# Keeping six of eight split weight blocks for the last two token tiles of an output product

## The chip, the cores and the metric

The kernel runs on one core of one Trainium2 chip. The metric is the device time of one execution in microseconds, taken as the median of several runs. Five engines work side by side: PE multiplies matrices, ACT and DVE work elementwise, POOL does small leftovers, and SP issues the transfers between HBM and the on-chip memory (SBUF). Each takes its instructions in the order that the built program fixed for it, and waits for the others by semaphores. Products accumulate in PSUM.

## The reference

The reference is a two-layer encoder on 1024 tokens of width 1024 in float32. Layer 0 mixes tokens by two kinds of attention, layer 1 by a gated linear recurrence; both end in a dense gated feed-forward part. The change touches only the last step of each mixer and the norm behind it:

```python
m = concat(out_a, out_b) @ w_out          # layer 0: attn_w_out, 1024 x 1024
m = (hs * gate) @ w_out                   # layer 1: rg_w_out,   1024 x 1024
x = x + rmsnorm(m, norm_mix_post[layer])
h = rmsnorm(x, norm_ffn_pre[layer])
f = (silu(h @ w_gate) * (h @ w_up)) @ w_down
```

Results have to agree with float32 products, so no operand may simply be rounded.

## The kernel before

There are eight token tiles of 128 tokens (0 to 7), and eight weight blocks of 128 x 1024 per `w_out` (one for each 128 rows of the sum).

**Two ways to multiply.** A product of two float32 operands is made in one of two ways. In the first, each operand is cut into a high part (a cast to the `F32R` type, on ACT) and a low part (operand minus high part, on DVE), and PE makes three passes: high x high, high x low, low x high. In the second, PE multiplies the plain float32 rows; the trace then shows two records for each such product of 128 x 512. `split` (L140) cuts a weight block: the cast is L155 (tile `whi`), the subtraction L156 (`wlo`). `split_act` (L581) cuts the activations: L582 (`ah`), L583 (`al`). All products of the stage are recorded on L572.

**The output product, `out_product` (L555).** A first pass makes tiles 0, 1, 2, a second makes tiles 3, 4, 5; each loads and splits all eight weight blocks anew, and keeps three PSUM tiles open at once (`pst`, three buffers, so the second pass can begin only when the tile-0 result has been read out of its buffer). The list `kept` remembers the split parts of the last four blocks of the second pass. Tiles 6 and 7 come last: the four kept blocks in three passes, and then, for tile 6 and after it for tile 7, the other four blocks as plain rows, loaded once more (L634).

**Rings.** Loaded weight blocks go through a ring of three buffers, `raw` (L136): a load waits until the subtraction of the block three before it is done. Split parts go through a ring of eight, `w`, which so holds four blocks. Activations (`act`, `ah`, `al`) have rings of three. The plain rows of the tail and then the first seven weight operands of the feed-forward part (`q`, made by `gate_load`: casts L691, subtractions L692) take the same ring `w` in turn.

**The norm.** When a tile's product is complete, `post_norm_of` squares it (ACT L178, tile `junk`), multiplies by the gain (DVE L250, `mg<-ps`; with that, PSUM is free), takes the root on POOL (`rs`, L182 and L183), adds the residual (DVE L256, `x`), and writes `x` out. `pre_norm` squares that again (ACT L178, `mg<-x`), takes the root on POOL, and scales (ACT L212, `mg<-x,rs`). PE then turns the tile in eight 128 x 128 transposes (L222), and ACT and DVE spread the turned tile into the operands `hS` of the feed-forward part (L85, L89, L96).

**Order.** The engines' order is made when the program is built, by a simulation of the timeline that places each instruction when it would be ready; `behind` adds that an instruction may not be placed ahead of another. So an edit can change the order on all engines. In the tail, the transposes of tiles 3, 4, 5 are placed ahead of the first three plain blocks of tile 6, and the first products of the feed-forward part (`first`, then `strassen`, L721 to L723) fill the time in which tiles 6 and 7 are normed.

## Time and profile before

| | us |
|---|---|
| runs, median of 3 | 2201.48 |
| lowest, highest | 2198.03, 2202.87 |
| the profiled execution | 2197.6 |
| its span, first to last instruction | 2195.8 |
| PE busy | 2161.5 |
| DVE busy | 1540.4 |
| ACT busy | 1170.8 |

The stage of the output product lies at 486 to 600 us for layer 0 and at 1455 to 1569 us for layer 1. A row of the timeline gives start, duration, engine, line, operation, the tiles (out<-in, without their numbers), shapes and a count; what stands in brackets is how long the engine was idle before, and what it waited for. A PE row's duration contains the time in which the next instruction already runs; the pitch of PE is the distance of starts.

### The profile page before, as it was taken

To read this page: it belongs to the slowest core of one execution; us is meant where nothing else is said; L and a number is where in the kernel's file an instruction comes from. 1 tells how busy PE (TensorE), PEld (TensorE's weight loads), DVE (VectorE), ACT (ScalarE), POOL (GpSimd) and SP (SyncE) were. 2 spreads that over 40 slices of the span, in tenths; PEclk is the share of its full clock that TensorE was granted. 3 is DMA by queue.
4 is the path that set the end of the run, shared out by engine and by line. 5 is a ranking of instruction groups with operands and counts; after the bars stand their busy time and mean duration, and the time that the engine had idled before them with its cause. 6 is when DMAs were issued, how large, how long until landed. Compare 5 with 4: busy or idle time off the path is not lost. (4 is left out here: it accounts for less than half of the span.)

```text
span 2195.8 us, 30592 instructions
## 1 busy us (share of the span) xinstructions
PE 2161.5 (98%) x11140; PEld 1802.7 (82%) x11140; DVE 1540.4 (70%) x2526; ACT 1170.8 (53%) x2174; POOL 219.3 (10%) x450
## 2 busy tenths in 40 slices
PE   9999999999999999999999999999999999999998
PEld 8888889878788888888887777888788888888886
DVE  5877865556878777776777677437787777758675
ACT  6655555556765544443446676528754444424443
POOL 2111113121100000000002333102000000000011
PEclk9999999999999999999999999999999999999999
DMA  7101011126323333236458411356233333328565
GB/s 273 34 30 49 24 40 49 54 95 210 137 91 112 123 97 112 89 126 229 145 179 256 131 59 39 95 197 219 90 118 105 100 116 91 117 96 289 171 182 154
DMA packets 168279, 270.21 MB, mean 123 GB/s; under 512 B 13889, under 2 KB 94785, under 8 KB 168129
## 3 DMA queue, kind: packets, MB, share of 16 engines
q1 hardware_dynamic: 167488, 266.18, 37.7%
q10 hardware_dynamic: 640, 2.10, 0.3%
q8 instruction: 87, 1.43, 0.3%
q14 instruction: 64, 0.52, 0.1%
HBM read 202.69 MB, written 65.54 MB: 122 GB/s over the span
## 5 line engine op out<-in xcount | busy, mean ns | idle before, releaser
L722 PE MATMUL ps<-hS,q 128*128 128x512 f32 (+1 forms) x1288 | 490.0, 381 | 0.9 <-DVE hS L89 0.9
L721 PE MATMUL ps<-hS,q 128*128 128x512 f32 (+1 forms) x1288 | 490.3, 381 | 0.4 <-ACT hS L96 0.4
L723 PE MATMUL ps<-hS,q 128*128 128x512 f32 (+1 forms) x1288 | 489.2, 380 | 0.0
L692 DVE TENSOR_TENSOR q<-raw,q 128x512 fp32r<-128x512 f32 x308 | 204.7, 686 | 183.8 <-ACT q L691 183.3
L722 PEld LDWEIGHTS ps<-hS,q 128*128 128x128 f32 x1288 | 242.9, 189 | 47.5 <-DVE hS L89 1.3
L721 PEld LDWEIGHTS ps<-hS,q 128*128 128x128 f32 x1288 | 242.4, 189 | 47.0 <-ACT hS L96 0.8
L723 PEld LDWEIGHTS ps<-hS,q 128*128 128x128 f32 x1288 | 242.9, 189 | 46.1
L691 ACT CAST q<-raw 128x512 fp32r<-128x512 f32 x308 | 177.7, 616 | 160.9 <-DVE raw L700 123.2
L807 PE MATMUL ps<-o,o 128*128 128x512 f32 x616 | 240.0, 390 | 0.2
L808 PE MATMUL ps<-o,o 128*128 128x512 f32 x616 | 238.0, 390 | 0.5 <-DVE o L936 0.5
L679 ACT ACTIVATE raw<-raw,gcol 128x256 f32<-128x256 f32 x352 | 150.3, 498 | 145.1 <-DMA raw<-in_ffn_w_up_dram 77.6
L806 PE MATMUL ps<-o,o 128*128 128x512 f32 x616 | 221.3, 391 | 3.6 <-ACT o L935 2.7
L801 ACT CAST o<-raw 128x512 fp32r<-128x512 f32 x184 | 110.6, 620 | 159.3 <-PE ps L808 56.7
L182 POOL TENSOR_SCALAR rs<-ss 128x1 f32<-128x1 f32 x52 | 25.0, 481 | 1429.1 <-ACT junk L178 1363.7
L802 DVE TENSOR_TENSOR o<-raw,o 128x512 fp32r<-128x512 f32 x184 | 123.3, 687 | 54.8 <-ACT o L801 54.2
L806 PEld LDWEIGHTS ps<-o,o 128*128 128x128 f32 x616 | 115.5, 188 | 30.0 <-ACT o L935 4.5
L808 PEld LDWEIGHTS ps<-o,o 128*128 128x128 f32 x616 | 115.6, 188 | 25.1 <-DVE o L936 1.3
L807 PEld LDWEIGHTS ps<-o,o 128*128 128x128 f32 x616 | 115.7, 188 | 24.9 <-DVE o L802 1.0
L156 DVE TENSOR_TENSOR wlo<-raw,whi 128x1024 fp32r<-128x1024 f32 x76 | 93.3, 1228 | 57.7 <-ACT whi L155 57.0
L409 DVE TENSOR_TENSOR_SCAN pr<-pr,zero 128x128 f32<-128x128 f32 (+7 forms) x64 | 86.9, 1361 | 30.7 <-POOL pr L406 25.7
L155 ACT CAST whi<-raw 128x1024 fp32r<-128x1024 f32 x76 | 79.7, 1050 | 49.2 <-PE ps L167 20.1
L166 PE MATMUL psq<-hT,whi 128*128 128x512 f32 x256 | 101.8, 398 | 0.1
(206 smaller groups left out, 4315.8 us busy)
## 6 DMA issues: line engine op xcount, KB each, us to landing
raw<-in_ffn_w_gate_dram SPq DMA_DIRECT2D x44, 512.0 KB, 4.2
raw<-in_ffn_w_up_dram SPq DMA_DIRECT2D x44, 512.0 KB, 4.2
gS<-c SPq DMA_DIRECT2D x88, 256.0 KB, 3.9
raw<-gS SPq DMA_DIRECT2D x88, 256.0 KB, 2.7
gA<-c SPq DMA_DIRECT2D x66, 256.0 KB, 3.3
raw<-in_ffn_w_down_dram SPq DMA_DIRECT2D x63, 256.0 KB, 4.4
raw<-gA SPq DMA_DIRECT2D x44, 256.0 KB, 2.8
t<-in_ffn_w_down_dram SPq DMA_DIRECT2D x22, 512.0 KB, 6.5
```

Source lines behind the costliest of these rows:

```text
L166: nc.tensor.matmul(ps, wh[:, kt, cols], hh[:, kt, :], start=kt == 0, stop=False)
L679: nc.scalar.activation(raw[:, i], raw[:, i], AF.Copy, scale=gain[:, 4 * k + i:4 * k + i + 1])
L691: self.last = nc.scalar.copy(t[:, 0], src).ins
L692: self.last_lo = nc.vector.tensor_tensor(t[:, 1], src, t[:, 0].bitcast(F32), op=ALU.subtract).ins
L721: nc.tensor.matmul(ps, a[:, 0, kt, :], bh, start=kt == 0, stop=False)
L722: nc.tensor.matmul(ps, a[:, 0, kt, :], bl, start=False, stop=False)
L723: self.matmul = nc.tensor.matmul(ps, a[:, 1, kt, :], bh, start=False, stop=kt == 3).ins
L801: nc.scalar.copy(t[:, 0], src)
L802: tt(t[:, 1], src, t[:, 0].bitcast(F32), op=ALU.subtract)
L806: nc.tensor.matmul(ps, a[0], b[:, 0], start=first, stop=False)
L807: nc.tensor.matmul(ps, a[0], b[:, 1], start=False, stop=False)
L808: nc.tensor.matmul(ps, a[1], b[:, 0], start=False, stop=last)
```

## The change

The second pass puts the split parts of blocks 3 and 4 of its order (`kts[2:4]`) into a new ring of four, `more`, in a pool of its own, and `kept` now remembers every block. Tiles 6 and 7 take the four last blocks as before, then the two blocks of `more` in three passes, with two more activations split for it, and only the first two blocks as plain rows. Two loads of 512 KB per layer fall away. Lines move by one behind L139 and by five or six behind the tail: L155 is L156 in the changed kernel, L178 is L179, L250 is L251, L691 is L696.

```diff
--- before.py
+++ after.py
@@ -137,9 +137,10 @@
         self.last_load = self.nc.sync.dma_start(raw.rearrange("p (a b) -> p a b", a=a), src).ins
         return raw
 
-    def split(self, src, a, b, gain=None, raw=None, pool=False):
-
-        nc, m = self.nc, self.main
+    def split(self, src, a, b, gain=None, raw=None, pool=False, home=None):
+
+        nc = self.nc
+        m, tag, bufs = home or (self.main, "w", 8)
         if raw is None:
             raw = self.raw(src, a)
         if gain is not None and pool:
@@ -150,8 +151,8 @@
             v = raw.rearrange("p (a b) -> p a b", a=a)
             nc.vector.tensor_tensor(v, v, gain.rearrange("p (a o) -> p a o", o=1).to_broadcast([P, a, b]),
                                     op=ALU.mult)
-        hi = m.tile([P, 1024], F32R, tag="w", bufs=8, name=self.uid("whi"))
-        lo = m.tile([P, 1024], F32R, tag="w", bufs=8, name=self.uid("wlo"))
+        hi = m.tile([P, 1024], F32R, tag=tag, bufs=bufs, name=self.uid("whi"))
+        lo = m.tile([P, 1024], F32R, tag=tag, bufs=bufs, name=self.uid("wlo"))
         nc.scalar.copy(hi, raw)
         nc.vector.tensor_tensor(lo, raw, hi.bitcast(F32), op=ALU.subtract)
         return (hi.rearrange("p (a b) -> p a b", a=a),
@@ -552,7 +553,7 @@
     def psum_t(self):
         return self.pt.tile([P, 512], F32, tag="tr", bufs=2, name=self.uid("pst"))
 
-    def out_product(self, ap, pp, first, aT, w, x_src, x_dst, gpost_v, sink, kts):
+    def out_product(self, ap, more, pp, first, aT, w, x_src, x_dst, gpost_v, sink, kts):
 
         nc = self.nc
         wv = [w[kt * P:(kt + 1) * P, :].rearrange("p (a b) -> p a b", a=2) for kt in range(KT)]
@@ -582,7 +583,7 @@
             nc.scalar.copy(ah, a)
             nc.vector.tensor_tensor(al, a, ah.bitcast(F32), op=ALU.subtract)
 
-        gpost, kept = None, []
+        gpost, kept = None, {}
         for t0 in (0, 3):
             pst = [psum() for _ in range(3)]
             for kt in kts:
@@ -595,8 +596,8 @@
                 else:
                     a = act(kt, t0, 3, ap, 3)
                     ah, al = (ap.tile([P, 384], F32R, tag=n, bufs=3, name=self.uid(n)) for n in ("ah", "al"))
-                wh, wl = self.split(wv[kt], 2, 512)
-                kept = kept[-3:] + [(wh, wl)]
+                wh, wl = self.split(wv[kt], 2, 512, home=(more, "more", 4) if t0 and kt in kts[2:4] else None)
+                kept[kt] = wh, wl
                 split_act(a, ah, al)
                 for t in range(3):
                     tok = slice(t * P, (t + 1) * P)
@@ -620,25 +621,29 @@
 
 
         pst = [psum() for _ in range(2)]
-        for i, (kt, (wh, wl)) in enumerate(zip(kts[4:], kept)):
+        def passes(kt):
             a = act(kt, 6, 2, ap, 3)
             ah, al = (ap.tile([P, 384], F32R, tag=n, bufs=3, name=self.uid(n))[:, :2 * P] for n in ("ah", "al"))
             split_act(a, ah, al)
+            wh, wl = kept[kt]
+            return [(ah, wh), (ah, wl), (al, wh)]
+
+        for i, kt in enumerate(kts[4:]):
+            ps_of = passes(kt)
             for t in range(2):
                 tok = slice(t * P, (t + 1) * P)
                 with self.behind([self.matmul] if t else ()):
-                    matmuls(pst[t], [(ah[:, tok], wh), (ah[:, tok], wl), (al[:, tok], wh)], i == 0, False)
-        rows, acts = [], []
-        for i, kt in enumerate(kts[:4]):
+                    matmuls(pst[t], [(x[:, tok], y) for x, y in ps_of], i == 0, False)
+        tail = [passes(kt) for kt in kts[2:4]]
+        for kt in kts[:2]:
             raw = self.main.tile([P, 2, 512], F32, tag="w", bufs=8, name=self.uid("raw"))
             nc.sync.dma_start(raw, wv[kt])
-            rows.append(raw)
-            acts.append(act(kt, 6, 2, ap, 3, ("act", "act", "act", "ah")[i]))
+            tail.append([(act(kt, 6, 2, ap, 3), raw)])
         for t in range(2):
             for i in range(4):
 
                 with self.behind([self.matmul] + ([self.turned[3 + i]] if t == 0 and i < 3 else [])):
-                    matmuls(pst[t], [(acts[i][:, t * P:(t + 1) * P], rows[i])], False, i == 3)
+                    matmuls(pst[t], [(x[:, t * P:(t + 1) * P], y) for x, y in tail[i]], False, i == 3)
             if t == 0:
                 rest = norm(6, pst[0])
                 last_m = self.last_m
@@ -1143,8 +1148,8 @@
         nc.sync.dma_start(self.gcol, io["gcol"])
         with pool("s0") as sp:
             hS = HiddenS(self, sp)
-            with pool("o0", "right") as ap, psum("po0") as pp:
-                self.out_product(ap, pp, lambda *a: first(0, *a), oT,
+            with pool("o0", "right") as ap, pool("more0") as more, psum("po0") as pp:
+                self.out_product(ap, more, pp, lambda *a: first(0, *a), oT,
                                  io["attn_w_out"], x, xs[0], io["norm_mix_post"][0],
                                  hS, [4, 5, 6, 7, 0, 1, 2, 3])
             if stop == 0:
@@ -1168,8 +1173,8 @@
             banks.close()
         with pool("s1") as sp:
             hS = HiddenS(self, sp)
-            with pool("o2", "right") as ap, psum("po2") as pp:
-                self.out_product(ap, pp, lambda *a: first(1, *a), yT,
+            with pool("o2", "right") as ap, pool("more2") as more, psum("po2") as pp:
+                self.out_product(ap, more, pp, lambda *a: first(1, *a), yT,
                                  io["rg_w_out"], xs[1], xs[2], io["norm_mix_post"][1],
                                  hS, list(range(KT)))
             if stop == 2:
```

The edit moves instructions in both layers in the same way. Three places in layer 0 follow; the numbers at the names tell the tiles apart.

On ACT, where the first pass ends. `whi` is a weight block's cast, `ah` an activation's, and `junk<-ps` the squaring of tile 0, with which the reading of the first PSUM tile begins. Before:

```order
L155 CAST whi_5986<-raw_5984 128x1024
L582 CAST ah_5982<-act_5980 128x384
L155 CAST whi_6016<-raw_6014 128x1024
L582 CAST ah_6012<-act_6010 128x384
L155 CAST whi_6046<-raw_6044 128x1024
L178 ACTIVATE junk_5870,ss_5872<-ps_5624 128x1024
```

Now:

```order
L156 CAST whi_5989<-raw_5987 128x1024
L156 CAST whi_6049<-raw_6047 128x1024
L583 CAST ah_5985<-act_5983 128x384
L156 CAST whi_6019<-raw_6017 128x1024
L156 CAST whi_6079<-raw_6077 128x1024
L583 CAST ah_6015<-act_6013 128x384
L156 CAST whi_6109<-raw_6107 128x1024
L179 ACTIVATE junk_5873,ss_5875<-ps_5627 128x1024
```

Ahead of the squaring of tile 0 stood the cast of the second pass's third block; there stands now the cast of its fifth (`raw_6107`), and the third and fourth are cast earlier.

On SP, the loads for these casts. Before:

```order
L137 DMA raw_6044<-in_attn_w_out_dram 128x1024
L562 DMA act_6040<-oT_79 128x384
L137 DMA raw_6074<-in_attn_w_out_dram 128x1024
L562 DMA act_6070<-oT_80 128x384
L137 DMA raw_6104<-in_attn_w_out_dram 128x1024
L562 DMA act_6100<-oT_73 128x384
```

Now:

```order
L137 DMA raw_6047<-in_attn_w_out_dram 128x1024
L563 DMA act_6043<-oT_79 128x384
L137 DMA raw_6077<-in_attn_w_out_dram 128x1024
L137 DMA raw_6107<-in_attn_w_out_dram 128x1024
L563 DMA act_6073<-oT_80 128x384
L137 DMA raw_6137<-in_attn_w_out_dram 128x1024
```

The fifth block's load (`raw_6104`, now `raw_6107`) stands in the same place among the weight loads; only an activation load has gone behind it.

On DVE, between the gain of tile 6 (`mg<-ps`) and its residual (`x<-mg,rs,x`). Before:

```order
L250 TENSOR_TENSOR mg_6454<-ps_6356,g_5865 128x1024
L705 TENSOR_TENSOR raw_6486<-raw_6486,raw_6480 128x4x128
L89 TENSOR_TENSOR hS_5617<-tf_6314,hS_5616 128x16x64
L256 SCALAR_TENSOR_TENSOR x_6455<-mg_6454,rs_6458,x_6455 128x1024
```

Now:

```order
L251 TENSOR_TENSOR mg_6469<-ps_6359,g_5868 128x1024
L710 TENSOR_TENSOR raw_6509<-raw_6509,raw_6503 128x4x128
L697 TENSOR_TENSOR q_6519<-raw_6503,q_6519 128x512
L89 TENSOR_TENSOR tf_6317<-tf_6317,mg_6233 128x256
L697 TENSOR_TENSOR q_6520<-raw_6509,q_6520 128x512
L257 SCALAR_TENSOR_TENSOR x_6470<-mg_6469,rs_6473,x_6470 128x1024
```

Two subtractions of the feed-forward weights and a small step of the turning have come in between, and one larger step (`hS<-tf`) has gone out.

## The prediction

> **What bounds the kernel now.** I read the page's span and busy times first, then the waits of PE.

> ```profile
> span 2195.8 us, 30592 instructions
> PE 2161.5 (98%) x11140; PEld 1802.7 (82%) x11140; DVE 1540.4 (70%) x2526; ACT 1170.8 (53%) x2174; POOL 219.3 (10%) x450
> PE pst L222 <- ACT mg L212: 4.8, 3, 2.0
> PE ps L806 <- ACT o L935: 2.7, 4, 1.2
> ```

> PE is busy all the time, and its longest waits are three for a scaled tile ahead of its transposes, 4.8 us together. So every microsecond taken from PE counts, unless it comes back as a wait, and every new wait of PE counts in full. The timeline of PE at the end of layer 0's stage gives prices:

> ```profile
> 565.15 1.04 PE L222 MATMUL pst<-ident,mg 128*128 128x128 f32 x8
> 566.03 1.88 PE L572 MATMUL ps<-raw,act 128*128 128x512 f32 x4
> 567.75 1.04 PE L222 MATMUL pst<-ident,mg 128*128 128x128 f32 x8
> 568.62 1.88 PE L572 MATMUL ps<-raw,act 128*128 128x512 f32 x4
> 571.21 10.47 PE L572 MATMUL ps<-raw,act 128*128 128x512 f32 x24
> 582.83 0.28 PE L723 MATMUL ps<-hS,q 128*128 128x256 f32 x1
> 585.08 1.09 PE L222 MATMUL pst<-ident,mg 128*128 128x128 f32 x8 [1.98 <-ACT mg L212]
> ```

> Tile 3's transposes start at 565.15; the plain blocks of tiles 6 and 7 follow, then products of the feed-forward part, then 1.98 us of nothing until tile 6 is normed. One plain block of one tile is four records, 567.75 - 566.03 = 1.72 us.

> The other place that matters is the end of the first pass: ACT, DVE, SP and PE, and the landing of a load in the window 512 to 516 and in 520 to 526.

> ```profile
> 510.99 1.05 ACT L155 CAST whi<-raw 128x1024 fp32r<-128x1024 f32 x1
> 514.65 0.52 ACT L582 CAST ah<-act 128x384 fp32r<-128x384 f32 x1 [2.61 <-PE ps L572]
> 515.07 1.05 ACT L155 CAST whi<-raw 128x1024 fp32r<-128x1024 f32 x1
> 516.24 1.02 ACT L178 ACTIVATE junk<-ps 128x1024 bf16<-128x1024 f32 x1
> ...
> 512.07 1.23 DVE L156 TENSOR_TENSOR wlo<-raw,whi 128x1024 fp32r<-128x1024 f32 x1 [0.39 <-ACT whi L155]
> 516.15 1.23 DVE L156 TENSOR_TENSOR wlo<-raw,whi 128x1024 fp32r<-128x1024 f32 x1 [0.40 <-ACT whi L155]
> 517.38 1.23 DVE L250 TENSOR_TENSOR mg<-ps,g 128x1024 f32<-128x1024 f32 x1
> ...
> 513.32 0.33 SPq L137 DMA_DIRECT2D raw<-in_attn_w_out_dram  x1
> ...
> 518.53 0.39 PE L572 MATMUL ps<-whi,al 128*128 128x512 f32 x1
> 518.75 0.41 PE L572 MATMUL ps<-whi,ah 128*128 128x512 f32 x1
> ...
> raw<-in_attn_w_out_dram SPq DMA_DIRECT2D x1, 512.0 KB, 3.7
> raw<-in_attn_w_out_dram SPq DMA_DIRECT2D x1, 512.0 KB, 5.1
> ```

> The second pass's first product (518.75) needs tile 0's PSUM, which DVE frees at 517.38 + 1.23 = 518.61. PE does not wait, but with 0.14 us to spare. The casts repeat every 515.07 - 510.99 = 4.08 us, a block of 18 passes (three tiles, two halves, three), so a pass costs 0.227 us.

> **The change part by part.**

> *PE.* A block of one tile in three passes is six passes, 1.36 us, against 1.72 as plain rows: 0.36 less. Two blocks and two tiles make 1.44 us per layer, 2.9 us in both. That is all the direct gain there is.

> *The loads taken away.* Two of 512 KB per layer; no PE row above waits for them, so they cost nothing now. I price them at 0; the low end would be a wait that the list of PE's waits does not have.

> *The end of the first pass.* ACT takes its queue in order: at 514.65 it had stood 2.61 us for an activation buffer with ready work behind. The third block's cast (515.07) stood ahead of tile 0's squaring (516.24) and waited for nothing. Now the fifth block's cast stands there. Its load, the one issued at 513.32, cannot go sooner: it waits for its buffer, which the subtraction 512.07 to 513.30 frees, and that one follows the cast of 510.99, which still stands behind the activation cast of that block. Landing takes 3.7 us here, so the cast begins at 517.0 instead of 515.07, and the squaring, the new block's subtraction, the gain and the freed PSUM follow 1.9 us later, at about 520.5. PE, which had 0.14 us to spare, stands still for about 1.9 us. Before, the first pass's squarings, gains and residuals lay between this load and its cast and hid it; with that cover gone it is on the path. Bounds: 0 if the load landed by 515, 3.3 with the landing of 5.1 us (513.32 + 5.1 - 515.07). I take 1.9, since 3.7 is this very load's landing, and the other loads now issued close by come behind it. Queued behind the waiting cast are the squarings of tiles 0 and 1; DVE's gain and POOL's root wait for these. What follows on ACT, DVE and POOL moves with PE, by the same amount. One more wait could come of it: the first feed-forward weight's scaling now stands on ACT ahead of the fourth block's activation cast. I take 0 and allow 0.7 at the high end, the difference of the two landings halved.

> *The tail.* Two blocks of tile 6 shrink, so its product ends 0.72 us sooner, and PE has 0.72 us less of tile 7 to cover its norm. When the norm ends decides, since the transposes wait for it already. These rows follow it: ACT, then DVE, then the whole stretch.

> ```profile
> 558.75 0.39 ACT L582 CAST ah<-act 128x256 fp32r<-128x256 f32 x1
> 563.13 1.12 ACT L691 CAST q<-raw 128x512 fp32r<-128x512 f32 x2
> 564.16 1.06 ACT L178 ACTIVATE mg<-x 128x1024 f32<-128x1024 f32 x1
> 567.00 1.15 ACT L212 ACTIVATE mg<-x,rs 128x1024 f32<-128x1024 f32 x1
> 574.85 1.02 ACT L178 ACTIVATE junk<-ps 128x1024 bf16<-128x1024 f32 x1 [0.70 <-PE ps L572]
> 580.52 1.05 ACT L178 ACTIVATE mg<-x 128x1024 f32<-128x1024 f32 x1
> 583.88 1.15 ACT L212 ACTIVATE mg<-x,rs 128x1024 f32<-128x1024 f32 x1 [2.21 <-POOL rs L183]
> ...
> 576.00 1.22 DVE L250 TENSOR_TENSOR mg<-ps,g 128x1024 f32<-128x1024 f32 x1
> 577.14 0.68 DVE L705 TENSOR_TENSOR raw<-raw,raw 128x512 f32<-128x512 f32 x1
> 577.74 1.22 DVE L89 TENSOR_TENSOR hS<-tf,hS 128x1024 fp32r<-128x1024 f32 x1
> 578.87 1.28 DVE L256 SCALAR_TENSOR_TENSOR x<-mg,rs,x 128x1024 f32<-128x1024 f32 x1
> ...
> 566.00:582.00 16.00, 16.00 (x55) 8.25 (x54) 15.69 (x29) 13.01 (x23) 2.00 (x4) 1.00 0.46 179
> ```

> In the last row DVE is busy 15.69 of 16 us and ACT had only 0.70 us of idle before it squared tile 6. The change adds two activation casts to ACT (0.39 each) and two subtractions to DVE. Thus 0.78 of new work eats the 0.70, and a product that ends 0.72 sooner finds ACT still busy. Tile 5's squaring (564.16) also goes behind both casts of the new activations and its scaling (567.00) comes about a microsecond later, with part of ACT's queue behind it. So tile 6's squaring starts 0.1 (0.78 - 0.70) to 0.9 us later than at 574.85; I take 0.5. Then DVE: between gain and residual lay 577.14 to 578.87, 1.73 us; now two weight subtractions of the size of the one at 577.14 (0.60 each, to 577.74) and a step of half that size (0.3, an estimate) replace the 1.13 of the large one (577.74 to 578.87), so +0.4. Scaling and transposes: +0.9 against tile 3's transposes, instead of -0.72. Tile 7's residual now stands behind the large step (1.13), partly covered: +0.3. The tail thus comes out 1.2 us longer per layer, its 1.44 us of PE work turned into idle time before tile 6's transposes (1.98 becomes about 4). Bounds: -1.44 if the norm keeps up with everything, +1.9 with 0.9, 0.4 and 0.6.

> *Sum.* 1.9 + 1.2 = 3.1 us per layer. Layer 1 has the same order and nearly the same rows, so 6.2 in all: 2197.6, the profiled execution, becomes 2203.8. That execution ran 3.9 us under the median of the runs, 2201.48, so I add the 6.2 to the median: 2207.7.

> **The clock.** Behind the 1.98 us gap of layer 0 the granted clock fell; behind the same gap in layer 1 it did not:

> ```profile
> 586.00:590.00 4.00, 4.00 (x23) 4.00 (x22) 3.85 (x4) 3.97 (x8) 0.79 (x2) 0.57 0.19 76
> 1554.00:1558.00 4.00, 4.00 (x36) 4.00 (x35) 3.15 (x3) 3.97 (x9) 0.79 (x2) 1.00 0.20 69
> ```

> With the clock at 0.57, 23 products instead of 36 were begun in 4 us: 13 x 0.11 = 1.4 us lost. A new gap of 1.9 us inside dense work could cost this in each layer, 2.8 in all, by chance of its position; I leave it out of the sum and keep it for the range.

> [...]

> **The rivals.**

> *No stall at the end of the first pass* (0.20). The load lands by 515. For it: landings of about 3.7 leave only 1.9 us to find. Against it: its buffer is freed at 513.30. Then only the tail counts: 2 x 1.2 = 2.4, 2203.9.

> *The tail follows the product* (0.12). The norm keeps its length and starts 0.72 sooner. For it: ACT has waits in the tail that earlier free operand buffers take away. Against it: DVE at 15.69 of 16. With the stall: 2 x (1.9 - 0.72) = 2.4, again 2203.8.

> *Faster* (0.06). One mechanism: operand buffers of the feed-forward part come free before the tail rather than after plain blocks, so the norm gets so short that PE's gap closes. It decides from the point where the norm shortens by more than the 0.72 us of cover that is lost. Then PE's 1.44 and most of the 1.98 us go per layer, without a stall: 2 x -3.4 = -6.8, 2194.7. PE's 2.9 alone would give 2198.6, which is within the bound below.

> *The clock falls too* (0.20, a part of slower). Both stalls fall badly: 6.2 + 2.8 = 9.0, 2210.5.

> **How the numbers follow.** 0.2% of 2201.48 is 4.4 us, about what a measurement of this kernel can tell from no change. The forecast (2207.7, 6.2 slower) has 0.42 and the clock's case 0.20: slower 0.62. The two rivals at +2.4 have 0.32: same. Faster 0.06. The likeliest case's own range is 2204 to 2211. The range for 8 in 10 reaches down over the rivals at +2.4, with the runs' own spread of 2 to 3 us, to 2200.5, and up to the long landing (2 x 3.3 + 2.4 = 9.0) with one fallen clock (1.4) and some spread, 2213.

> **What would show it.** Right: a PE wait for DVE's `mg` of about 1.9 us at the first product of the second pass in both layers; ahead of it on ACT a `whi` cast that waits for the load of a weight block; plain rows x32 instead of x64; tile 6's transposes waiting some 4 us. Wrong: no wait of PE at that product, or a gap before the transposes of 2.7 us or less, which would mean that the norm followed its product.

## The result, and the profile after

The change makes the kernel slower, by little: 2204.74 us (median of 20 runs) against 2198.82 us for the kernel before on the same chip, a ratio of 1.0031 with a 95% interval of 1.0025 to 1.0036. By the medians that is 5.9 us, by the ratio 6.8 (5.5 to 7.9). Forecast was a difference of 6.2, on a median of 2201.48 for the kernel before, so 2207.7. That is 3.0 us too much, of which 2.7 come from the starting point: the median of the first three runs lay that much above the one of 20. The profiled execution took 2202.89 us. Its page begins:

```profile
span 2201.1 us, 30616 instructions
PE 2162.0 (98%) x11156; PEld 1808.3 (82%) x11156; DVE 1541.6 (70%) x2530; ACT 1172.8 (53%) x2178; POOL 219.4 (10%) x450
```

PE idles 2201.1 - 2162.0 = 39.1 us, before 2195.8 - 2161.5 = 34.3: 4.8 more. PE is busy 0.5 us longer, although it has less to do. Where the idle time went, the list of PE's waits says (waited for: us in all, times, longest):

```profile
PE pst L223 <- ACT mg L213: 4.5, 2, 2.5
PE pst L223 <- ACT mg L85: 4.2, 3, 3.1
```

The first row is the old wait, the scaled tile ahead of its transposes. The second is new: transposes that wait for a free PSUM buffer, which a copy on ACT (L85) empties. The rows of PE for the transposes of tiles 3 to 7 show where, layer 0 first, then layer 1; the last number is the idle time ahead. After:

```profile
565.50 1.03 PE L223 MATMUL pst<-ident,mg 128*128 128x128 f32 x8
568.53 1.15 PE L223 MATMUL pst<-ident,mg 128*128 128x128 f32 x8 [0.63 <-ACT mg L85]
571.50 1.14 PE L223 MATMUL pst<-ident,mg 128*128 128x128 f32 x8 [0.43 <-ACT mg L85]
586.23 1.64 PE L223 MATMUL pst<-ident,mg 128*128 128x128 f32 x8 [2.55 <-ACT mg L213]
594.68 1.10 PE L223 MATMUL pst<-ident,mg 128*128 128x128 f32 x8
...
1534.69 1.03 PE L223 MATMUL pst<-ident,mg 128*128 128x128 f32 x8
1536.94 1.03 PE L223 MATMUL pst<-ident,mg 128*128 128x128 f32 x8
1542.47 1.97 PE L223 MATMUL pst<-ident,mg 128*128 128x128 f32 x8 [3.12 <-ACT mg L85]
1558.20 1.10 PE L223 MATMUL pst<-ident,mg 128*128 128x128 f32 x8 [1.97 <-ACT mg L213]
1566.64 1.09 PE L223 MATMUL pst<-ident,mg 128*128 128x128 f32 x8
```

And before, the last of these in layer 0, then the first and the last in layer 1:

```profile
593.25 1.03 PE L222 MATMUL pst<-ident,mg 128*128 128x128 f32 x8
...
1533.85 1.04 PE L222 MATMUL pst<-ident,mg 128*128 128x128 f32 x8
...
1561.43 1.09 PE L222 MATMUL pst<-ident,mg 128*128 128x128 f32 x8 [0.80 <-ACT mg L212]
```

From tile 3's transposes to tile 7's, "the tail" below, layer 0 took 593.25 - 565.15 = 28.10 us and takes 29.18; layer 1 took 27.58 and takes 31.95. Layer 1 carries most of it (4.37 of 5.45 us), by a wait of 3.12 us ahead of tile 5's transposes that layer 0 does not have. The rows of DVE, POOL and ACT there, and the same place in layer 0 (last two rows):

```profile
1536.06 3.23 POOL L183 TENSOR_SCALAR rs<-ss 128x1 f32<-128x1 f32 x1 [4.99 <-ACT mg L179]
...
1538.53 0.68 DVE L705 TENSOR_TENSOR raw<-raw,raw 128x512 f32<-128x512 f32 x1
1541.67 0.69 DVE L89 TENSOR_TENSOR hS<-mg,hS 128x512 fp32r<-128x512 f32 x1 [2.46 <-ACT hS L96]
...
1539.98 1.15 ACT L213 ACTIVATE mg<-x,rs 128x1024 f32<-128x1024 f32 x1 [3.05 <-POOL rs L184]
...
568.09 0.22 POOL L183 TENSOR_SCALAR rs<-ss 128x1 f32<-128x1 f32 x1 [6.17 <-ACT mg L179]
...
568.51 0.92 DVE L89 TENSOR_TENSOR tf<-mg 128x256 f32<-128x256 f32 x2 [0.50 <-ACT mg L85]
```

POOL's operation on 128 x 1 numbers, the first half of the root for tile 5's second norm, takes 0.22 us in layer 0 and 3.23 in layer 1. In layer 1 it ends at 1539.29, right after DVE has run dry (1538.53 + 0.68 = 1539.21); in layer 0 DVE had a pause of 0.50 us just then. ACT's scaling stands for that root, ACT's copies stand behind the scaling, and PE's transposes wait for the copies. A run of DVE without a pause does not always do this, though. In the kernel before, the same operation for tile 5 lay in such a run too and took 0.47 us:

```profile
565.39 0.47 POOL L182 TENSOR_SCALAR rs<-ss 128x1 f32<-128x1 f32 x1 [3.85 <-ACT mg L178]
```

The clock is the second part. In the rows for stretches of the change (length and PE's busy time, products begun, granted clock) the clock is 0.50 in layer 1 too, where before it stayed at 1.00 (in the trace's clock records from 589.8 to 2190.7 us):

```profile
1542.40:1545.80 3.40, 3.33 (x10) 0.50 0.00 0
1545.80:1549.20 3.40, 3.40 (x11) 1.00 0.00 0
1559.40:1562.80 3.40, 3.40 (x19) 0.50 0.00 0
```

With layer 0's fall, which the kernel before has as well (0.50 from 586.4 to 589.8), that is two falls more. At a clock of 0.50, 3.4 us cost 1.7 us, an estimate from these two numbers, so 3.4 in all. The account closes: 4.8 of idle time, 3.4 of clock, and 2.9 less work on PE give +5.3 us, which is the difference of the spans. The runs bear the clock's part out: the mean granted clock of the change's 20 runs is 0.9954, and that of the kernel before is 0.9969 to 0.9971 in the four series of runs beside the experiments. The difference of some 0.0016 is 3.5 us of 2200.

### The profile page after: what moved, and what is told of

Read it like the earlier page. It is cut to its first block, busy times and chain, and to the rows that moved or that the text cites. A ratio compares the mean times of both kernels' runs of the same rounds, so it can differ in the third digit from the quotient of the medians.

```text
span 2201.1 us, 30616 instructions
## 1 busy us (share of the span) xinstructions
PE 2162.0 (98%) x11156; PEld 1808.3 (82%) x11156; DVE 1541.6 (70%) x2530; ACT 1172.8 (53%) x2178; POOL 219.4 (10%) x450
## 5 line engine op out<-in xcount | busy, mean ns | idle before, releaser
L696 ACT CAST q<-raw 128x512 fp32r<-128x512 f32 x308 | 178.3, 616 | 178.4 <-DVE raw L705 131.6
L806 ACT CAST o<-raw 128x512 fp32r<-128x512 f32 x184 | 110.6, 620 | 158.0 <-PE ps L813 47.5
L183 POOL TENSOR_SCALAR rs<-ss 128x1 f32<-128x1 f32 x52 | 26.5, 509 | 1435.1 <-ACT junk L179 1362.9
L156 ACT CAST whi<-raw 128x1024 fp32r<-128x1024 f32 x76 | 79.7, 1050 | 50.1 <-PE ps L168 20.4
## 6 DMA issues: line engine op xcount, KB each, us to landing
raw<-in_ffn_w_gate_dram SPq DMA_DIRECT2D x44, 512.0 KB, 4.1
raw<-in_ffn_w_up_dram SPq DMA_DIRECT2D x44, 512.0 KB, 4.2
t<-in_ffn_w_down_dram SPq DMA_DIRECT2D x22, 512.0 KB, 6.5
```

The lines of the kernel that those rows point to most:

```text
L696: self.last = nc.scalar.copy(t[:, 0], src).ins
L806: nc.scalar.copy(t[:, 0], src)
```

## The experiments

The differences in us below are (ratio - 1) x 2198, with the 95% interval in brackets.

**One layer at a time.** `out_product` exists twice, as before and as changed:

```
 layer 0:  self.out_product(ap, more, pp, ...)      # e1: changed;  e2: as before
 layer 1:  self.out_product_b(ap, pp, ...)          # e1: as before; e2: changed
```

> The change in layer 0 alone; layer 1's output product is as before. Theory S (the root of tile 5 on POOL, held up behind DVE in layer 1, and what follows from it carries the loss): in the profile of the change layer 1 starts only 0.3 us late, so +0 to +1 us against the kernel before, no difference that can be measured. Rival R (the prediction's: each layer loses the same at the end of the first pass and in the tail): half of the change's loss, +3 us.

> The change in layer 1 alone; layer 0's output product is as before. Theory S: the whole loss, +4 to +6 us, with a wait of PE of about 3 us for a copy on ACT (L85) ahead of tile 5's transposes in layer 1, and one POOL operation of some 3 us there. Rival R: +3 us, like layer 0 alone.

Layer 0 alone: +1.3 us [-0.7, 3.3]. Layer 1 alone: +4.4 [2.6, 6.4], with 3.17 us of waiting ahead of tile 5's transposes and 3.24 us for POOL's operation. The intervals do not quite exclude halves; the profiles, with the wait in layer 1 only, speak for theory S.

**Without tile 5's root.** In `pre_norm`, `rstd` returns the plain mean square for tile 5:

```
+        if not root:
+            return ss[-1]
```

> The change in both layers, with the two POOL operations left out that take the root for tile 5's second norm: tile 5 is scaled with its plain mean square, so its numbers are wrong from there, while every other instruction and its order on PE, DVE, ACT and SP is that of the change. Theory S: ACT no longer waits 3.05 us for POOL ahead of tile 5's scaling in layer 1, PE's wait of 3.12 us goes and with it the fallen clock right behind it (about 1.4 us): +0.5 to +2 us against before. Rival R: the root of tile 5 is beside the path, so the loss stays, +5 to +6 us.

```profile
1537.58 1.03 PE L225 MATMUL pst<-ident,mg 128*128 128x128 f32 x8
1539.84 1.03 PE L225 MATMUL pst<-ident,mg 128*128 128x128 f32 x8
1542.26 1.14 PE L225 MATMUL pst<-ident,mg 128*128 128x128 f32 x8
1556.99 1.09 PE L225 MATMUL pst<-ident,mg 128*128 128x128 f32 x8 [2.55 <-ACT mg L215]
1565.43 1.09 PE L225 MATMUL pst<-ident,mg 128*128 128x128 f32 x8
```

These are tiles 3 to 7 in layer 1. The wait is gone, and the tail takes 1565.43 - 1537.58 = 27.85 us, within 0.3 of the kernel before. But the time was +5.5 us [3.1, 7.9], where 0.5 to 2 had been expected. So the root accounts for the tail of layer 1 and not for the whole loss. The mean granted clock of these runs is 0.9954, as low as the change's, and 0.9970 for the kernel before beside them, so about 3.5 of the 5.5 us lie in the clock, and leaving out the root did not bring them back. What else stands in this profile is a wait of 1.3 us for the gain at the end of layer 1's first pass: the prediction's third step, which the one profile of the change had shown with 0.28 us only. It was in every profile that has the change's loads in layer 1. In the run with a product put ahead (e6, below) it looked like this, by rows of ACT, of PE, and of a stretch of time:

```profile
1485.30 1.05 ACT L156 CAST whi<-raw 128x1024 fp32r<-128x1024 f32 x1 [2.36 <-DMA raw<-in_rg_w_out_dram]
...
1488.79 0.80 PE L573 MATMUL ps<-whi,ah 128*128 128x512 f32 x1 [2.61 <-DVE mg L251]
...
1488.20:1495.00 6.80, 6.21 (x15) 0.50 0.71 259
```

There ACT stood 2.36 us for the fifth block's load ahead of tile 0's squaring, PE 2.61 us, and then the clock was at 0.50 for 6.8 us, which costs another 3.1 by estimate (half of the 6.21 us of work in them).

**The sums of the weights later, and the first half alone.** The first puts three sums on DVE behind tile 4's differences, so that DVE pauses. The second (e5) keeps the blocks in their own buffers, with the tail of the kernel before.

```
 e4: +        with self.behind([self.gap] if behind else ()):
                  tt(a22, a21, a22, op=ALU.add)      # and the two behind it
 e5: -        tail = [passes(kt) for kt in kts[2:4]]
     +        rows, acts = [], []                    # four blocks as plain rows
```

> The change, with the three sums of the first feed-forward weights (L703 to L705 of the change) put on DVE behind tile 4's differences, and what depends on them behind tile 6's norm: DVE then runs dry for a moment after tile 3's transposes, as in layer 0 of the change. Theory S: POOL's root gets through there, the wait ahead of tile 5's transposes goes in layer 1, and tile 6's norm finds ACT and DVE freer: 3 to 6 us less than the change, -1 to +2 us against before. Rival R: sums that come later delay the weights' parts, so nothing is won, +5 us or more.

> The first half of the change alone: the second pass keeps the parts of its third and fourth block in buffers of their own, so the ring's buffers come free earlier, and the tail is that of the kernel before, with four blocks as plain rows. Theory S (the end of the first pass costs little; the tail's new casts and subtractions on ACT and DVE carry the loss): a wait of PE for the gain of 0.3 to 1.4 us at the end of layer 1's first pass, as in the four profiles with the change there, none in layer 0, no wait of 3 us ahead of tile 5's transposes; 0 to +2 us against before. Rival E (earlier weights alone crowd DVE: the feed-forward weights' parts come earlier and hold up tile 5's root): +3 to +5 us with the wait of 3 us in layer 1.

The sums later: +7.9 us [5.1, 10.6]. Tile 5 no longer waits (0.55 us), but the weights' parts now stand around tile 6's norm, and POOL's root waits there:

```profile
1557.77 3.77 POOL L183 TENSOR_SCALAR rs<-ss 128x1 f32<-128x1 f32 x1 [4.60 <-ACT mg L179]
...
1559.57 1.89 DVE L698 TENSOR_TENSOR q<-raw,q 128x512 fp32r<-128x512 f32 x3
...
1563.42 1.97 PE L223 MATMUL pst<-ident,mg 128*128 128x128 f32 x8 [5.23 <-ACT mg L213]
```

POOL is done at 1561.54, DVE's run ends at 1561.46, and PE has stood for 5.23 us. The theory of the root held; the cure only moved the wait.

The first half alone: +2.2 us [0.0, 4.4], with 1.1 us of waiting at the end of layer 1's first pass and none in layer 0, as expected of theory S. A held-up root appeared here too, that of tile 3's second norm, in both layers. Two more roots stand behind it on POOL, ACT waits 1.75 us for the last of them before it scales tile 4, and PE waits 1.82 us ahead of tile 4's transposes:

```profile
1531.34 2.96 POOL L183 TENSOR_SCALAR rs<-ss 128x1 f32<-128x1 f32 x1 [2.76 <-ACT mg L179]
...
1533.80 0.42 DVE L89 TENSOR_TENSOR tf<-tf,mg 128x256 f32<-128x256 f32 x1
1534.26 1.22 DVE L251 TENSOR_TENSOR mg<-ps,g 128x1024 f32<-128x1024 f32 x1
```

The root ended at 1534.30, at DVE's pause between 1534.22 and 1534.26.

**A product ahead of tile 6's transposes.** The first pause of the 256-wide products is moved behind the second product, in the change, in the kernel before, and in the change with the sums behind tile 4's first difference:

```
-        yield self.matmul
         p2 = product("A12", 1)
+        yield self.matmul
```

> The change, with one more feed-forward product (twelve products of 256 columns, 1.4 us) ahead of tile 6's transposes on PE, for tile 6 and tile 7 alike: the order of PE's queue alone is set otherwise. Theory S (PE's gap ahead of tile 6's transposes is the price of the norm, and the clock falls behind it): the 2.55 us gap becomes about 1.1 us in both layers, and the falls behind it go (about 1.5 us each): 2 x 1.4 + 1 to 2 falls = 4 to 6 us less than the change, +1 to +3 us against before with the wait in layer 1 ahead of tile 5 still there. Rival G (what is put ahead is missed behind: the last products need tile 7's parts, and the gap opens there): as the change, +5 us or more.

> The kernel before with the same order of PE's queue. Theory S: the gap of 1.98 us becomes 0.6 in both layers, and the fallen clock behind it in layer 0 goes: 2 x 1.4 + 1.5 = about 4 us less, -3 to -5 us against before. Rival G: 0 us.

> The change with that order of PE's queue, and with the three sums of the first feed-forward weights put on DVE behind the first difference of tile 4, which stands after tile 3's copies: DVE has a pause there, in which POOL's root of tile 5 can run. Theory S: no wait of 3 us ahead of tile 5's transposes in layer 1, so 3 us less than the change with the new order of PE alone; -3 to 0 us against before. Rival (as with the sums put later, where the wait moved to tile 6's transposes): the gap ahead of these is 4 us or more, and the time is that of the change or worse.

In the change: +6.4 us [3.7, 8.8], nothing won. The gap ahead of tile 6's transposes fell to 0.38 us, but 1.52 us opened ahead of tile 7's and up to 0.96 ahead of later products, and the end of the first pass had its wait of 2.61 us. In the kernel before: +2.0 [-0.7, 4.6]. The second product there waits for ACT's copy of the first, which shares its PSUM buffer and stands behind the scaling of tile 6:

```profile
1556.37 0.39 PE L721 MATMUL ps<-hS,q 128*128 128x256 f32 x1 [3.24 <-ACT first L727]
```

So rival G held: what is put ahead waits itself, or is missed behind. With the sums moved as well: +8.8 [5.9, 11.6]. Tile 5 no longer waits long (0.44 us in layer 1), but the time is no better than the change's, as the rival said; tile 6's gap is 2.70 us and not the 4 or more it named, and 2.30 us opened ahead of tile 7.

**The cast put behind, and both waits away.** The fifth block's cast and subtraction go behind tile 1's squaring and gain, where they stood before the change; other instructions around the first pass's end change places with them. The second run leaves out tile 5's root too.

```
+                with self.behind(last_m if t0 and kt == kts[4] else ()):
                     wh, wl = self.split(wv[kt], 2, 512, home=...)
```

> The change, with the fifth block's cast and subtraction in the second pass put behind tile 1's squaring (ACT) and tile 1's gain (DVE), as the order was before the change. Theory P (the prediction's third step, seen in layer 1 alone: in seven profiles PE waits there 0.3 to 2.7 us for the gain, 1.5 on average, with the clock fallen behind the two longest): that wait of PE is gone, 1.5 to 3 us less than the change, +3 to +5 us against before, with the wait of 3 us ahead of tile 5's transposes still there. Rival (what the cast no longer holds up is held up one block later, by the fourth and fifth block's products): +5 to +7 us, as the change.

> The same, and tile 5 scaled with its plain mean square, so that its root on POOL is left out (its numbers are wrong from there). Theory: the two waits of layer 1 together carry the loss, so with both away 0 to +2 us against before, and PE's only longer wait in the tails is that ahead of tile 6's transposes. Rival (the loss is the fallen clock and the tail of layer 0, wherever the waits are): +4 us or more.

With the cast behind: +4.8 us [2.9, 6.8], 2.0 less than the change's 6.8, as theory P had it, though the intervals overlap. PE has no wait at the first pass's end there, and the one ahead of tile 5 (3.17 us) stays. With both away: +0.9 us [-1.1, 2.9], no difference that can be measured. Waits of PE in this kernel, the two longest groups first:

```profile
PE pst L225 <- ACT mg L215: 5.1, 2, 2.5
PE ps L814 <- ACT o L943: 3.5, 4, 2.0
...
PE ps L729 <- DVE first L738: 1.5, 1, 1.5
```

Of the transposes in the tails only tile 6's wait long. A product behind them in layer 1 waits 1.46 us for DVE (third row), as it did with the cast behind alone. So the two waits of layer 1 together, with the clock behind them, account for the loss against the kernel before. They do not account for the 2.9 us that PE was to win: with both waits away the tails take 28.52 and 27.80 us, before 28.10 and 27.58, although PE has 1.44 us less to do in each. What is taken from PE there comes back, mostly as idle time.

One thing is open: taking away the root alone saved only 1.3 us, the cast alone 2.0, both together 5.9. The three intervals allow a plain sum. The clock may tie them together: its mean lies below the kernel before's by 0.0016 without the root, by 0.0008 with the cast behind and by 0.0003 with both away (3.5, 1.7 and 0.6 us). With 7 to 11 runs each, and a clock given to 0.001, this is a hint and no more. Whether leaving out the root gains something in the kernel before was not tried either; in its profile PE does not wait for it.

**Two versions to beat both.** The first has the cast behind and the product ahead; the second also scales tile 5 on DVE:

```
+        if later and t == 5:
+            self.scaled = nc.vector.tensor_scalar(h, x, rs, None, op0=ALU.mult).ins
```

> The change with the cast put behind, and with one more feed-forward product ahead of tile 6's transposes on PE (as in the run of that order). Theory: PE's gap ahead of tile 6's transposes is 0.4 us, tile 7's 1.5 us, the wait of layer 1's first pass is gone, the one ahead of tile 5 stays unless DVE pauses: +1 to +4 us against before. Rival: the wait for tile 5's root is set by when DVE has a pause, and moves with the order, so that it is gone or appears in layer 0: -2 us, or +6 us and more.

> The kernel with the cast put behind and the feed-forward product ahead of tile 6's transposes, and with tile 5's scaling on DVE instead of ACT, in both layers: DVE's queue then holds an instruction that needs POOL's root, so DVE itself pauses where before only ACT stood. Theory (POOL's root waits until DVE pauses): the root of tile 5 takes well under 1 us in both layers, the wait of 3 us ahead of tile 5's transposes is gone, at the price of about 1 us more of DVE ahead of tile 6's norm: 3 us less than the same kernel with the scaling on ACT, so -2 to +2 us against before. Rival (DVE, busy nearly all of the tail, loses with the scaling what the pause gives back at tile 6's transposes): +3 to +6 us, with a gap of 2 us or more ahead of tile 6's transposes.

With the scaling on ACT: +5.3 us [3.3, 7.5], with 3.12 us of waiting ahead of tile 5 still there; beside the cast behind alone (+4.8) the product ahead wins nothing. With the scaling on DVE: +2.0 [0.0, 4.0], 3.3 us less, as expected, though the intervals overlap a little:

```profile
1535.39 1.36 POOL L183 TENSOR_SCALAR rs<-ss 128x1 f32<-128x1 f32 x1 [4.99 <-ACT mg L179]
...
1537.44 0.75 DVE L213 TENSOR_SCALAR mg<-x,rs 128x1024 f32<-128x1024 f32 x1 [0.77 <-POOL rs L184]
...
1553.25 1.09 PE L225 MATMUL pst<-ident,mg 128*128 128x128 f32 x8 [0.31 <-ACT mg L215]
1561.90 1.09 PE L225 MATMUL pst<-ident,mg 128*128 128x128 f32 x8 [3.05 <-ACT mg L215]
```

DVE now stands for the root itself, 0.77 us, and POOL gets through in 1.36 us (more than the "well under 1" expected). Tiles 5 and 6 go without a long wait; tile 7's norm is late instead, by 3.05 us. No version beats the kernel before.

## Why the prediction came out as it did

The forecast difference of 6.2 us lies between the two measures of it, 5.9 and 6.8; but that agreement is in good part luck. Of the four stall terms in the sum only layer 0's tail came about as described and in its size. Both signs that the prediction had named for being wrong appeared, too: layer 0 has no wait at the second pass's first product, and the gap ahead of tile 6's transposes is below 2.7 us (2.55 and 1.97). The second was no good sign, since the norm did not follow its product; the first was.

*PE's direct gain, 2.9 us.* It holds. From tile 3's transposes to tile 4's, with one block of one tile between, PE took 567.75 - 565.15 = 2.60 us before and takes 1536.94 - 1534.69 = 2.25 in the change: 0.35 less, for 0.36 forecast. With it the account of the two profiles closes.

*The loads taken away, 0.* Nothing contradicts it: no new wait for a load of the plain rows appeared.

*The end of the first pass, 1.9 us in each layer.* This step failed in its assumption. It had the fifth block's load issued at 513.32 at the earliest, behind the second block's subtraction. But with buffers of their own the third block's cast and subtraction move ahead of the second's, and the fifth block's load goes out when the third's subtraction ends:

```profile
515.51 1.05 ACT L156 CAST whi<-raw 128x1024 fp32r<-128x1024 f32 x1 [0.17 <-DMA raw<-in_attn_w_out_dram]
...
509.88 1.23 DVE L157 TENSOR_TENSOR wlo<-raw,whi 128x1024 fp32r<-128x1024 f32 x1 [0.50 <-ACT whi L156]
...
509.41 2.06 SPq L137 DMA_DIRECT2D raw<-in_attn_w_out_dram  x2
```

The subtraction ends at 511.11, the second load of the last row goes out then, 2.2 us sooner than assumed, and the cast waits 0.17 us. That is the rival "no stall at the end of the first pass", and in layer 0 it holds in all profiles. In layer 1 the mechanism is there as described, a cast that waits for its load ahead of tile 0's squaring. There the third block's cast already waits for its own load, 1.78 us in the change and 3.94 in the run with a product put ahead, and the fifth block's load goes out later for it. But the size changes from one profile to the next: 0.28, 0.98, 1.3, 1.4, 1.1, 2.61 and 2.7 us in seven profiles, 1.5 on average. Putting the cast behind took it away. So the term is 0 + 1.5 on this average instead of 1.9 + 1.9, too large by some 2.3 (in the change's own profile 0 + 0.28).

*The tail, +1.2 us in each layer.* In layer 0 it holds: tile 6's transposes start 20.73 us behind tile 3's where it was 19.93, so +0.80 for a predicted +0.9, and tile 7's +1.08 for +1.2. The gap ahead of tile 6 became 2.55 us and not 4, since part of the delay (0.63 + 0.43) already appears ahead of tiles 4 and 5. In layer 1 the step failed. With tile 5's root away its tail is 0.2 to 0.3 us longer than before, for 1.2 forecast; with it, 4.4. "Layer 1 has the same order and nearly the same rows, so 6.2 in all" was the sentence at fault: the same order without DVE's pause of 0.50 us (in layer 0 ACT had stood 1.09 us for an activation load, and DVE for ACT) has another wait. That the pause makes the difference between the layers fits the rows, but no run shows it alone. A row of the profile before hinted at such a wait, POOL's operation of 0.22 us in a dense stretch of DVE (here tile 6's root), and the prediction did not price it:

```profile
581.76 1.29 POOL L182 TENSOR_SCALAR rs<-ss 128x1 f32<-128x1 f32 x1 [4.83 <-ACT mg L178]
```

*The clock.* It was left out of the sum and kept as a rival at 1.4 us a fall. Two falls more, 1.7 each by the estimate above, are in the profile. Together with the root, which the prediction did not see, this made up for what the first pass's end and layer 1's own tail did not cost. The sum is right by luck.

*The rivals.* The tail did not follow the product, and nothing became faster: gaps of PE stayed and grew. The rival of the clock, which put the time at 9.0 us slower, had the falls right and the stalls wrong.

## What to carry to other kernels

A small operation on POOL that sat in a chain, the first half of a root on 128 x 1 numbers, took 0.22 us in a pause of DVE and 2.96 to 3.77 us in several profiles where DVE ran without one, though not in every such run (0.47 us in the kernel before). Before the order changes in a stretch where DVE is full already, look for the POOL rows in it that take longer than the same operation elsewhere (in the kernel before 1.29 us at 581.76, for 0.22 at 576.05). A load's time of issue follows from when its buffer is freed in the new order, not in the old one (here 511.11, not 513.32), so it must be worked through again step by step. Two stages with the same instructions need not react in the same way: here the change cost 1 us in the tail of one and 4 in that of the other, and the visible difference between them was a pause of half a microsecond. Work that is taken from an engine wins nothing where the same engine then waits longer for another: here PE had 2.9 us less to do and stood idle for 4.8 us more.

## What was not expected of the hardware

*A small operation on POOL took up to 3.77 us beside a run of DVE instructions.* In the profiles above POOL's 128 x 1 operation took 2.96 to 3.77 us inside an unbroken run of DVE, and ended within 0.1 us of that run's end (1539.29 for 1539.21, 1561.54 for 1561.46, 1534.30 in a pause of 0.04 us). In layer 0 of the change, in DVE's pause from 568.01 to 568.51, it took 0.22 us. Up to six borders between two instructions of DVE lie within the long ones, as from 1536.06 to 1539.29. Elsewhere it ended at the first border (0.68 us at 558.31 in the change, between two instructions that follow each other without a pause). What decides between the two is open, and no run shows why the operation takes longer. It is not the instructions around it alone: tile 3's root in layer 1 starts 0.68 us behind the same DVE instruction and has the same six instructions of DVE behind it in the change and in the first half alone, and takes 0.68 us in the one and 2.96 in the other.

*The clock falls by whole stretches of 3.4 us, and position decides.* These are stretches of PE in the change (first two rows, with waits of 3.12 and 1.97 us in them) and in the run with layer 1 alone (last three, with a wait of 3.17 us):

```profile
1539.00:1542.40 3.40, 0.35 (x2) 0.99 0.13 53
...
1556.00:1559.40 3.40, 1.43 (x13) 1.00 0.83 242
```

```profile
1538.70:1542.10 3.40, 1.71 (x10) 1.00 0.42 171
1542.10:1545.50 3.40, 1.93 (x11) 1.00 0.00 0
1545.50:1548.90 3.40, 3.40 (x11) 1.00 0.00 0
```

```profile
1552.80:1556.20 3.40, 1.45 (x13) 1.00 0.86 284
1556.20:1559.60 3.40, 3.40 (x30) 1.00 0.12 52
```

In the profiles of the kernel before and of the change, from 30 to 2180 us, every stretch of that grid at full clock with at most 1.44 us of work was followed by a fall (between the grid's exact borders 0.41, 0.86 and 1.44 us in the change, 1.44 before), and none of the others, which have 1.77 us or more. The 1.45 us of the run with layer 0 alone, without a fall, lie just above.
